# A hybrid block on one core: the gating branch ahead of the attention, its two projections as products of 2x2 blocks

## The chip, the core and the metric

One core of a Trainium2 chip runs the whole kernel. The time is device microseconds of one execution; the number for a kernel is the median of its runs. The engines are TensorE (PE, with its weight loads PEld), VectorE (DVE), ScalarE (ACT), GpSimd (POOL) and SyncE (SP), whose queue issues all the DMAs of this kernel.

## The reference

One layer over 512 positions of 1024 channels, all in float32. The parts that matter here:

```python
h = rmsnorm(x, norm_mix_g)
z = einsum('bsd,dc->bsc', h, w_in)              # 1024 -> 7184 columns
uv = gelu(z[..., :2048]); z_u, z_v = uv[..., :1024], uv[..., 1024:]
q, k, v, f_logit = ...                          # 3 x 1024 columns, 16 columns
gate_a, gate_b = split(sigmoid(z[..., 5136:]))  # 2 x 1024 columns
a = z_u * (mask(w_s) @ layernorm(z_v) + b_s)    # blocks of 128 positions, 8 groups
b = forgetting_attention(q, k, v, f_logit, b_f) # 16 heads, causal, cumsum of log sigmoid
x = x + (gate_a * (a @ w_a) + gate_b * (b @ w_b)) @ w_out
```

A gated MLP with a causal convolution, an embedding add and a last norm follow; the change doesn't touch them.

## The kernel before

Every product of the projections keeps float32 accuracy by a split. An operand is cast to the PE's float32r format (`hi`, on ACT) and the rest is subtracted (`lo`, on DVE or POOL); three matmuls (hi·lo, lo·hi, hi·hi) stand for one. `load_w` does it for a weight tile of 512 KB: a DMA into a `raw` buffer, the cast (L127), the subtraction (L128). `hT` holds the normed input, transposed and split, in two slots. A projection of 512 columns is four row blocks by 8 contraction tiles by 3 = 96 matmuls of 128x512.

PE's order is the program's (written out by hand in blocks, or by the order of the code). The other engines' order is set by a scheduler from the same code, and each engine then executes its queue strictly in order. A ring gives the weight buffers: 5 pairs of `whi`/`wlo` and 3 of `raw`. A load is issued on SP when its raw buffer is free. PSUM has 8 banks, in tags that rotate; a matmul that starts a bank waits until its last content has been read.

The stages: (1) x is normed in four blocks (`rms_x`, with `gmix`, the norm's weights copied to all partitions by POOL, L336) and transposed into hT, while PE does the embedding's product (`pp`) and the first half of V (`pv`). (2) The forget gate's 16 matmuls (L410) and its cumsum, a scan of nine steps on DVE (L424, L425). (3) The second half of V (`proj_N`, 96 matmuls). (4) Attention by 8 pairs of heads, with the projections of q and k and 13 of the 16 gate tiles woven in; the gates go to DRAM (`gate_d`). (5) The zv projection (192 matmuls), layernorm of zv on DVE and POOL (L693 to L696), the zu projection (192). (6) The w_b phase, with the remaining gates and the mix of group g (`mix`: 3 matmuls with w_s, 4 transposes, into `aT`) between its tiles; then w_a, w_out and the rest.

Of the kernel before, what the change touches and what calls it, by code (L numbers as in the profile page):

```python
# [9 lines left out]
F32 = mybir.dt.float32  # L10
F32R = mybir.dt.float32r
# [4 lines left out]
P = 128  # L16
# [22 lines left out]
def hybrid_block(  # L39
# [27 lines left out]
    def uid(s):  # L67
        state["n"] += 1
        return f"{s}_{state['n']}"
# [26 lines left out]
    LATE = ("qy", "qt", "qh", "st", "mv", "va", "s0", "s1", "s2", "s3")  # L96
# [126 lines left out]

    ident = consts.tile([P, P], F32, tag="ident", name="ident")
# [89 lines left out]
    ring = open_ring("ring", 5)  # L314
# [10 lines left out]
    with tc.manual_schedule(engines={ET.PE, ET.Activation, ET.DVE, ET.SP}):  # L325
# [10 lines left out]
        G.partition_broadcast(gmix, grow)  # L336
# [60 lines left out]


    bft = consts.tile([P, 1], F32, tag="bft", name="bft")
    nc.sync.dma_start(bft[0:16, :], b_f.rearrange("o h -> h o"))  # L400

    wf_raw = scr.tile([P, 8, 64], F32, tag="wfr", name="wf_raw")
    wf2 = scr.tile([P, 8, 64], F32R, tag="wf2", name="wf2")
    nc.sync.dma_start(wf_raw, w_in_v[:, :, 5120:5184])
    V.tensor_copy(wf2, wf_raw)
    V.tensor_tensor(wf2[:, :, 32:48], wf_raw[:, :, 0:16], wf2[:, :, 0:16].bitcast(F32), ALU.subtract)
    bk = bank()
    for k in range(8):
        for t in (1, 0):
            T.matmul(bk[0:64, :], wf2[:, k, :], hT[t][:, k, :],  # L410
                     start=(k == 0 and t == 1), stop=(k == 7 and t == 0))
    fz = scr.tile([16, S], F32, tag="fz", name="fz")
    fa = scr.tile([16, S], F32, tag="fa", name="fa")
    fb = scr.tile([16, S], F32, tag="fb", name="fb")
# [16 lines left out]
    state["bank"] = 0  # L431
    proj_N(w_in_v[:, :, 4096:5120], 0, NK, hT, 1, evac_v, rb_outer=False)

# [5 lines left out]
    scr_es.close()  # L439
    psum.close()  # L440


    psum = open_psum("psumB", ATT_BANKS)
# [108 lines left out]


    gate_d = tc.dram_tile([N_EARLY * P, S], F32, name="gate_d")

    def gate_col(n):
        return (6160 if n < NK else 5136) + P * (n % NK)

    def gate_early(n):
        w = load_w(w_in_v[:, :, gate_col(n):gate_col(n) + P], 8, P, sub=None)  # L560
        bk = bank("mm")
        yield from proj_T_steps([(*w, 0, 8, 0)], hT, bk)
        t = att.tile([P, S], F32, tag="ot", name=uid("gt"), bufs=1)
        A.copy(t, bk)
        nc.sync.dma_start(gate_d[n * P:n * P + P, :], t)
# [6 lines left out]
    def run(g):  # L572
        for _ in g:
            pass

    def weave(items, fill, n):

        steps = len(items)
        done = 0
        for m, g in enumerate(items):  # L580
            next(g, None)
            while done < (m + 1) * n // steps:
                next(fill, None)
                done += 1

    def chain(*gs):
        for g in gs:
            yield from g

    with tc.manual_schedule(engines={mybir.EngineType.PE}):  # L590
# [3 lines left out]
        fill = chain(qk_pair(1, qk_weights(1), qk[1]), gate_early(0))  # L594
# [32 lines left out]
    state["pool"][5] = state["pool"][6] = state["pool"][7] = state["late"] = late  # L627
    scr_es, scr = open_pool("scrC", "right")

    zv = slot(5, F32).rearrange("p (b c) -> p b c", b=NB)  # L630

    def evac_zv(bk, rb, ch):
        state["zv"] = A.activation(zv[:, rb, 512 * ch:512 * ch + 512], bk, AF.Gelu_apprx_tanh)

    state["bank"] = 1
# [3 lines left out]
    prep = slot(7, F32)  # L639
    gb = prep[:, 1024:3072].rearrange("p (a c) -> p a c", a=2)  # L640
    nc.sync.dma_start(gb[:, 0, :], rows_bc(ln_g[0], D))
    nc.sync.dma_start(gb[:, 1, :], rows_bc(ln_b[0], D))


    wst = prep[:, 0:1024].rearrange("p (g s) -> p g s", g=8)
    nc.sync.dma_start(wst, w_s[0].rearrange("g t s -> t g s"))
    G.memset(wst[0:64, :, 64:128], 0.0)
    wsT = tuple(scr.tile([P, 8, P], F32R, tag=f"wsT{i}", name=f"wsT{i}") for i in range(2))
    for g0 in (0, 4):
        bk = bank()  # L650
        for g in range(4):
            T.transpose(bk[:, g * P:(g + 1) * P], wst[:, g0 + g, :], ident)
        split_out(wsT, bk.rearrange("p (g t) -> p g t", g=4),
                  (slice(None), slice(g0, g0 + 4), slice(None)))


    cvr = [prep[:, 3072 + P * i:3072 + P * i + P] for i in range(2)]
# [7 lines left out]
    nc.sync.dma_start(cvr[1][88:96, :], b_s[0])  # L665
    cvT = late.tile([P, 2 * P], F32, tag="cvT", name="cvT")
    late.tile([P, 32], F32, tag="gap", name="gap_late")
    bk = bank()
    for i in range(2):
        T.transpose(bk[:, i * P:(i + 1) * P], cvr[i], ident)  # L670
    V.tensor_copy(cvT, bk[:, :2 * P])
# [8 lines left out]
    def bs(g):  # L680
        return cvT[:, P + 88 + g:P + 89 + g]

    mv = tiny("mv", 2 * NB)
    va = tiny("va", NB)
    for rb in range(NB):
        st = tiny("st", 12)
        for h in range(2):
            V.bn_stats(st[:, 6 * h:6 * h + 6], zv[:, rb, 512 * h:512 * h + 512])
        V.bn_aggr(mv[:, 2 * rb:2 * rb + 2], st)
        V.tensor_scalar(va[:, rb:rb + 1], mv[:, 2 * rb + 1:2 * rb + 2], EPS, None, ALU.add)  # L690
    y = rsqrt_of(va, NB)
    for rb in range(NB):
        V.tensor_scalar(zv[:, rb, :], zv[:, rb, :], mv[:, 2 * rb:2 * rb + 1], y[:, rb:rb + 1],  # L693
                        ALU.subtract, ALU.mult)
        G.tensor_tensor(zv[:, rb, :], zv[:, rb, :], gb[:, 0, :], ALU.mult)
        G.tensor_tensor(zv[:, rb, :], zv[:, rb, :], gb[:, 1, :], ALU.add)  # L696

    zu = slot(6, F32).rearrange("p (b c) -> p b c", b=NB)

    def evac_zu(bk, rb, ch):  # L700
        A.activation(zu[:, rb, 512 * ch:512 * ch + 512], bk, AF.Gelu_apprx_tanh)

    oT = tuple(k_view(slot(i)) for i in (2, 3))
    with tc.issue_after(state["zv"].ins):
        for c in range(NK):
            split_out(oT, o32[:, c, :], (slice(None), c, slice(None)))
    aT = tuple(k_view(slot(i)) for i in (7, 4))

    def mix(g):
        c = slice(g * P, g * P + P)  # L710
        vh = scr.tile([P, NB, P], F32R, tag="vh", name=uid("vh"), bufs=1)
        vl = scr.tile([P, NB, P], F32R, tag="vl", name=uid("vl"), bufs=1)
        split_out((vh, vl), zv[:, :, c], (slice(None),) * 3)
        bk = bank()
        mm3(bk, wsT[0][:, g, :], wsT[1][:, g, :], vh, vl, True, True)
        an = scr.tile([P, NB, P], F32, tag="an", name=uid("an"), bufs=1)
        V.scalar_tensor_tensor(an, bk.rearrange("p (b c) -> p b c", b=NB), bs(g),
                               zu[:, :, c], ALU.add, ALU.mult)
        bk = bank()
        for n in range(NB):  # L720
            T.transpose(bk[:, n * P:(n + 1) * P], an[:, n, :], ident)
        split_out(aT, bk, (slice(None), g, slice(None)))

    for ch in range(2):
        proj_N(w_in_v[:, :, 0:1024], 0, NK, hT, ch, evac_zu, rb_outer=False)


    def gated(wv, act, n0):

        c0 = P * (n0 % NK)  # L730
        sgs = []
        for i in range(2):
            sg = scr.tile([P, S], F32, tag="sg", name=uid("sg"), bufs=2)
            if n0 + i < N_EARLY:
                nc.sync.dma_start(sg, gate_d[(n0 + i) * P:(n0 + i + 1) * P, :])
                src = sg
            else:
                src = bank()
                w = load_w(w_in_v[:, :, gate_col(n0 + i):gate_col(n0 + i) + P], 8, P)
                proj_T([(*w, 0, 8, 0)], hT, src)  # L740
            A.activation(sg, src, AF.Sigmoid)
# [263 lines left out]
```

## Time and profile before

| | before |
|---|---|
| median of 3 runs | 971.17 us (970.8 to 971.34) |
| profiled execution | 971.98 us, span 970.2 us |
| mean granted PE clock | 0.994 |
| PE busy | 946.9 us of the span |
| DVE, ACT, POOL busy | 559.6, 433.5, 139.3 us |
| moved by DMA | 110.72 MB, 114 GB/s |

The median is what counts as the time. The span runs from the first to the last instruction of the profiled execution. Busy time adds up the instructions' own durations, with what overlaps on an engine counted once.

### The profile page before, as it was taken

How to read it: one execution, taken by the hardware profiler on the slowest of the kernel's cores; microseconds unless marked ns; L12 is line 12 of the kernel's file. 1: busy time of each engine (PE TensorE's matmuls, PEld its weight loads, DVE VectorE, ACT ScalarE, POOL GpSimd, SP SyncE). 2: the span in 40 equal slices, each digit the busy share in tenths (PEclk: the TensorE clock that was granted, in tenths of full speed). 3: DMA queues.
4: the chain of work that ended last, by engine and by line, in shares of the span. 5: the costliest groups of instructions: out<-in, count | busy, mean ns of one | idle time of the engine just before them, and what ended most of it. 6: DMA issues, size and time to landing. Idle time of an engine off the chain costs nothing.

```text
span 970.2 us, 11655 instructions
## 1 busy us (share of the span) xinstructions
PE 946.9 (98%) x4422; PEld 785.1 (81%) x4422; DVE 559.6 (58%) x982; ACT 433.5 (45%) x721; POOL 139.3 (14%) x99
## 2 busy tenths in 40 slices
PE   6999999999999999999999999999999999999996
PEld 4778888878888888888888888888888888888885
DVE  4464877788852495454634756565356653365664
ACT  5355666666643353333423544343234341244443
POOL 1203222230000036000310400000000000000225
PEclk8999999999999999999999999999999999999998
DMA  5544433333236324556552333224223333223202
GB/s 184 174 118 145 114 102 99 98 94 101 90 98 178 109 65 130 161 165 212 184 200 66 112 119 95 87 87 130 88 66 111 106 109 89 85 87 124 72 22 87
DMA packets 96725, 110.72 MB, mean 114 GB/s; under 512 B 4821, under 2 KB 70541, under 8 KB 96670
## 3 DMA queue, kind: packets, MB, share of 16 engines
q1 hardware_dynamic: 96526, 109.72, 36.5%
q8 instruction: 35, 0.57, 0.3%
q10 hardware_dynamic: 144, 0.26, 0.1%
q14 instruction: 20, 0.16, 0.1%
HBM read 101.29 MB, written 8.68 MB: 113 GB/s over the span
## 4 chain that ended last, share of the span: by engine, by line
PE 91%; DVE 3%; POOL 2%; DMA 2%; issue 1%; ACT 1%; SPq 0%; POOLq 0%; DVEq 0%
PE bank L150 17%; PE bank L152 17%; PE bank L154 17%; PE bank L137 8%; PE bank L136 8%; PE bank L138 8%; PE bank L210 3%; PE bank L212 3%; PE bank L214 3%; PE bank L540 2%; PE bank L531 2%; DMA raw<-in_w_in_dram 2%; DVE t L520 1%; PE bank L503 1%; PE bank L269 1%
## 5 line engine op out<-in xcount | busy, mean ns | idle before, releaser
L150 PE MATMUL bank<-slot,wlo 128*128 128x512 f32 (+1 forms) x744 | 294.3, 397 | 0.0
L152 PE MATMUL bank<-slot,whi 128*128 128x512 f32 (+1 forms) x744 | 289.0, 389 | 0.0
L154 PE MATMUL bank<-slot,whi 128*128 128x512 f32 (+1 forms) x744 | 288.6, 388 | 0.0
L128 DVE TENSOR_TENSOR wlo<-raw,whi 128x1024 fp32r<-128x1024 f32 x132 | 173.7, 1318 | 139.8 <-ACT whi L127 139.3
L127 ACT CAST whi<-raw 128x1024 fp32r<-128x1024 f32 x156 | 163.2, 1047 | 175.8 <-PE bank L138 115.5
L154 PEld LDWEIGHTS bank<-slot,whi 128*128 128x128 f32 x744 | 139.6, 188 | 28.8
L150 PEld LDWEIGHTS bank<-slot,wlo 128*128 128x128 f32 x744 | 140.0, 188 | 23.7
L152 PEld LDWEIGHTS bank<-slot,whi 128*128 128x128 f32 x744 | 140.1, 188 | 22.3
L136 PE MATMUL bank<-whi,slot 128*128 128x512 f32 (+1 forms) x360 | 138.4, 385 | 0.0
L138 PE MATMUL bank<-whi,slot 128*128 128x512 f32 (+1 forms) x360 | 138.4, 384 | 0.0
L137 PE MATMUL bank<-wlo,slot 128*128 128x512 f32 (+1 forms) x360 | 138.4, 384 | 0.0
L128 POOL TENSOR_TENSOR wlo<-raw,whi 128x1024 fp32r<-128x1024 f32 x24 | 58.6, 2446 | 482.8 <-ACT whi L127 465.2
L136 PEld LDWEIGHTS bank<-whi,slot 128*128 128x128 f32 x360 | 67.6, 188 | 13.5
L138 PEld LDWEIGHTS bank<-whi,slot 128*128 128x128 f32 x360 | 67.6, 188 | 13.5
L137 PEld LDWEIGHTS bank<-wlo,slot 128*128 128x128 f32 x360 | 67.6, 188 | 13.3
L210 PE MATMUL bank<-whi,slot 128*128 128x512 f32 x152 | 60.3, 397 | 2.8 <-DVE slot L234 2.1
L212 PE MATMUL bank<-wlo,slot 128*128 128x512 f32 x152 | 59.3, 391 | 2.9 <-POOL wlo L128 2.9
L214 PE MATMUL bank<-whi,slot 128*128 128x512 f32 x152 | 59.7, 392 | 0.0
L845 DVE SCALAR_TENSOR_TENSOR ul<-bank,cvT,ul 128x511 f32<-128x511 f32 x22 | 16.5, 750 | 51.7 <-ACT ul L844 51.7
L234 DVE TENSOR_TENSOR slot<-bank,slot 128x512 fp32r<-128x512 f32 x42 | 27.9, 685 | 28.4 <-ACT slot L233 28.2
L513 ACT ACTIVATE t<-t,mn 128x512 f32<-128x512 f32 (+1 forms) x64 | 35.9, 562 | 11.7 <-DVE mn L510 7.9
L210 PEld LDWEIGHTS bank<-whi,slot 128*128 128x128 f32 x152 | 28.6, 188 | 9.9 <-DVE slot L234 3.3
(175 smaller groups left out, 1032.7 us busy)
## 6 DMA issues: line engine op xcount, KB each, us to landing
raw<-in_w_in_dram SPq DMA_DIRECT2D x56, 512.0 KB, 4.0
raw<-in_w_up_dram SPq DMA_DIRECT2D x44, 512.0 KB, 3.6
raw<-in_w_down_dram SPq DMA_DIRECT2D x22, 512.0 KB, 3.4
cum<-cum_d SPq DMA_DIRECT2D x8, 512.0 KB, 4.0
raw<-in_w_branch_b_dram SPq DMA_DIRECT2D x8, 512.0 KB, 4.6
raw<-in_w_branch_a_dram SPq DMA_DIRECT2D x8, 512.0 KB, 6.7
raw<-in_w_out_dram SPq DMA_DIRECT2D x8, 512.0 KB, 5.6
raw<-in_w_ple_gate_dram SPq DMA_DIRECT2D x8, 512.0 KB, 3.3
```

What stands on the lines that cost most here:

```text
L127: A.copy(hi, raw)
L128: (sub or V).tensor_tensor(lo, raw, hi.bitcast(F32), ALU.subtract)
L136: T.matmul(out_ap, alo, bhi, start=start, stop=False)
L137: T.matmul(out_ap, ahi, blo, start=False, stop=False)
L138: T.matmul(out_ap, ahi, bhi, start=False, stop=stop)
L150: T.matmul(out_ap, wl, ah, start=(n == 0 and k == 0), stop=False)
L152: T.matmul(out_ap, wh, al, start=False, stop=False)
L154: T.matmul(out_ap, wh, ah, start=False, stop=end)
L210: T.matmul(bk, alo[:, k, r], wh, start=(k == 0), stop=False)
L212: T.matmul(bk, ahi[:, k, r], wl, start=False, stop=False)
L214: T.matmul(bk, ahi[:, k, r], wh, start=False, stop=(k == nk - 1))
L513: A.activation(t, t, AF.Exp, scale=-1.0, bias=m, accum_out=rs[:, i:i + 1])
```

## The change

The gating branch moves ahead of the attention. Its two projections, zv and zu, 512x1024 by 1024x1024 each, are computed as 2x2 blocks by seven block products (Strassen's scheme in Winograd's form). The sums S1 to S4 of quarters of hT are made once, on POOL and DVE, and split. The sums of the weights' quarters are made on POOL in the raw buffers (`combine`, two operations 128x1024 for each of four sums and each projection); each product then has two weight tiles to cast (ACT) and subtract (DVE, `split_w`), and 24 matmuls into two banks (two row blocks, 4 contraction tiles, 3). Additions from PSUM on DVE put the products together.

The rest of the change follows from it. gmix comes by a DMA that repeats the row on all partitions, and POOL no longer does it. The first ring has 4 pairs and 8 raw buffers. The scan and the sums stand in the code ahead of V's second half. The layernorm's statistics are sums on ACT, its multiplication one DVE operation (L677) and its addition one POOL operation for each row block. The mix follows zu and is woven with three gate tiles; its `aT` goes to DRAM (`aT_d`) and is read back, 4 MB, behind the attention. The attention opens a new ring and new PSUM banks and weaves 12 gate tiles in; one more gate tile and the splits of the attention's output stand between it and the w_b phase, which reads all 16 gates from DRAM.

```diff
-GATES = [1, 2, 3, 4, 5, 6, 7, 10, 13]
-N_EARLY = GATES[-1]
+GATES = [4, 5, 6, 7, 8, 9, 10, 12, 15]
+N_MIX = GATES[0] - 1
+N_GATES = 2 * NK
+WINO_BANKS = {"c": 6, "f": 2}
...
+        t3 = lambda: combine((0, 1), (1, 1), (0, 1), ALU.subtract)
+        t2 = lambda: combine((0, 0), (0, 1), (0, 0), ALU.add)
+        t1 = lambda: combine((0, 1), (1, 1), (0, 0), ALU.subtract)
+        t4 = lambda: combine((1, 0), (1, 0), (0, 0), ALU.subtract)
...
+            (ready((0, 0), load), product("P1", act, 0, 0, "x", True)),
+            (ready((0, 1), t3), product("P7", sums[2], 0, 0, "z", True)),
+            (ready((0, 0), t2), product("P6", sums[1], 0, 0, "y", True)),
+            (ready((1, 0), t1), product("P2", act, 4, 0, "x", False)),
+            (ready((0, 1), t4), product("P5", sums[0], 0, 0, "y", False)),
+            (ready((1, 0)), product("P4", act, 4, 256, "z", False)),
+            (ready((1, 1)), product("P3", sums[3], 0, 0, "y", False)),
...
+            if name == "P1":
+                A.copy(c12, bk)
+            elif name == "P7":
+                V.tensor_tensor(c22, bk, c12, ALU.add)
...
-    ring = open_ring("ring", 5)
+    ring = open_ring("ring0", 4, 8)
...
-        grow = scr.tile([1, D], F32, tag="grow", name="grow")
-        nc.sync.dma_start(grow, norm_mix_g)
-        G.partition_broadcast(gmix, grow)
+        nc.sync.dma_start(gmix, rows_bc(norm_mix_g[0], D))
...
+    add_quarter(s1, a21, 1, 1, ALU.add)
+    split_out(sums[0], s1, full)
+    G.tensor_tensor(a21, a11, a21, ALU.subtract)
+    split_out(sums[2], a21, full)
...
+            V.scalar_tensor_tensor(zv[:, rb, :], zv[:, rb, :], y[:, rb:rb + 1], gb[0],
+                                   ALU.mult, ALU.mult)
+            G.tensor_tensor(zv[:, rb, :], zv[:, rb, :], gb[1], ALU.add)
+        steps(units, 120)
+        wsT = [quarter(f"S1{t}").rearrange("p (g t) -> p g t", g=8) for t in "hl"]
...
+        bk = bank("f")
+        T.transpose(bk[:, 0:P], bsr, ident)
+        V.tensor_copy(bsT, bk[:, 0:NK])
+        steps(units, 24)
...
+            for t in range(2):
+                nc.sync.dma_start(aT_d[t][g * P:g * P + P, :], ap[:, t].bitcast(F32))
...
+    ring = open_ring("ring", 5)
     psum = open_psum("psumB", ATT_BANKS)
...
-    proj_N(w_in_v[:, :, 1024:2048], 0, NK, hT, 0, evac_zv, rb_outer=False)
-    proj_N(w_in_v[:, :, 1024:2048], 0, NK, hT, 1, evac_zv, rb_outer=False)
...
-    for ch in range(2):
-        proj_N(w_in_v[:, :, 0:1024], 0, NK, hT, ch, evac_zu, rb_outer=False)
...
-        for g in range(c0 // P, c0 // P + 2):
-            mix(g)
```

The first place is DVE around V's second half. `slot_30` and `slot_31` hold V, and the four rows that write them from a bank are the evacuations of its row blocks; `fa` and `fb` before, and `mid_449` and `mid_450` now, are the scan's two tiles. Before:

```order
L128 TENSOR_TENSOR wlo_734<-raw_732,whi_733 128x1024 [waits DMAHW0_49,Activation_49]
L424 COPY fb<-fa 16x64 [waits DVE_49]
L425 TENSOR_TENSOR fb<-fa 16x448
L424 COPY fa<-fb 16x128 [waits DVE_49]
L425 TENSOR_TENSOR fa<-fb 16x384
L424 COPY fb<-fa 16x256 [waits DVE_49]
L425 TENSOR_TENSOR fb<-fa 16x256
L128 TENSOR_TENSOR wlo_740<-raw_738,whi_739 128x1024 [waits DMAHW1_49,Activation_49]
L234 TENSOR_TENSOR slot_30_135<-bank_515,slot_30_135 128x8x64 [waits Activation_49]
L234 TENSOR_TENSOR slot_30_135<-bank_516,slot_30_135 128x8x64 [waits Activation_49]
L234 TENSOR_TENSOR slot_31_136<-bank_517,slot_31_136 128x8x64 [waits Activation_49]
L234 TENSOR_TENSOR slot_31_136<-bank_518,slot_31_136 128x8x64 [waits Activation_49]
```

Now, with `zv_448` the scratch of the sums, `S4l` the low part of the sum S4, and `wlo_707` the low part of the second product's weights:

```order
L560 COPY mid_449<-mid_450 16x8 [waits DVE_49]
L561 TENSOR_TENSOR mid_449<-mid_450 16x504
L560 COPY mid_450<-mid_449 16x16 [waits DVE_49]
L561 TENSOR_TENSOR mid_450<-mid_449 16x496
L236 TENSOR_TENSOR wlo_707<-raw_688,whi_706 128x1024 [waits Activation_49]
L560 COPY mid_449<-mid_450 16x32 [waits DVE_49]
L561 TENSOR_TENSOR mid_449<-mid_450 16x480
L351 TENSOR_TENSOR slot_30_133<-bank_550,slot_30_133 128x8x64 [waits Activation_49]
L351 TENSOR_TENSOR slot_30_133<-bank_551,slot_30_133 128x8x64 [waits Activation_49]
L560 COPY mid_450<-mid_449 16x64 [waits DVE_49]
L561 TENSOR_TENSOR mid_450<-mid_449 16x448
L351 TENSOR_TENSOR slot_31_134<-bank_552,slot_31_134 128x8x64 [waits Activation_49]
```

The evacuations stood behind the scan and between weight splits; now the first two stand behind the sums and most of the scan, and the third, of `bank_552`, one scan step further on. The first product's second bank, `bank_715`, takes the place of `bank_552`.

The second place is DVE right behind the last step of the layernorm's inverse root (`qy`). Before, in the zu projection (`vl` is the first mix's):

```order
L693 TENSOR_SCALAR slot_626_2924<-slot_626_2924,mv_3215,qy_3237 128x1024 [waits DVE_49]
L693 TENSOR_SCALAR slot_626_2924<-slot_626_2924,mv_3215,qy_3237 128x1024 x3
L128 TENSOR_TENSOR wlo_3427<-raw_3425,whi_3426 128x1024 [waits DMAHW1_49,Activation_49]
L128 TENSOR_TENSOR wlo_3433<-raw_3431,whi_3432 128x1024 [waits DMAHW2_49,Activation_49]
L128 TENSOR_TENSOR wlo_3550<-raw_3548,whi_3549 128x1024 [waits DMAHW3_49,PE_49,Activation_49]
L128 TENSOR_TENSOR wlo_3556<-raw_3554,whi_3555 128x1024 [waits DMAHW4_49,Activation_49]
L234 TENSOR_TENSOR vl_3615<-slot_626_2924,vh_3614 128x512 [waits Activation_49]
```

Now, in zu's last two products; `wlo_1225` and `wlo_1229` are the weights of the last product, P3, `wlo_1318` and `wlo_1399` those of gates, and `S1l_1261` the low part of the transposed w_s:

```order
L677 SCALAR_TENSOR_TENSOR zv_671<-zv_671,qy_1053,mid_978 128x1024 [waits DMAHW6_49,DVE_49]
L677 SCALAR_TENSOR_TENSOR zv_671<-zv_671,qy_1053,mid_978 128x1024 x3
L236 TENSOR_TENSOR wlo_1225<-raw_930,whi_1224 128x1024 [waits DMAHW5_49,Activation_49]
L330 TENSOR_TENSOR slot_117_672<-bank_1124,slot_117_672 128x512 [waits PE_49]
L330 TENSOR_TENSOR slot_117_672<-bank_1125,slot_117_672 128x512 [waits PE_49]
L236 TENSOR_TENSOR wlo_1229<-raw_932,whi_1228 128x1024 [waits DMAHW6_49,Activation_49]
L130 TENSOR_TENSOR wlo_1318<-raw_1316,whi_1317 128x1024 [waits DMAHW3_49,Activation_49]
L333 TENSOR_TENSOR slot_117_672<-bank_1086,slot_117_672 128x512 [waits PE_49]
L333 TENSOR_TENSOR slot_117_672<-bank_1087,slot_117_672 128x512 [waits PE_49]
L130 TENSOR_TENSOR wlo_1399<-raw_1397,whi_1398 128x1024 [waits DMAHW4_49,Activation_49]
L351 TENSOR_TENSOR S1l_1261<-bank_1262,S1h_1260 128x512 [waits Activation_49]
```

PE's transpose of `bsr` writes the bank that `bank_1262` had, and stands in PE's order ahead of P3; so P3 stands behind the last of these rows. Before, no matmul of zu needed a bank whose reading stood behind the layernorm's rows.

The third place is SP at the start of the attention's loads. Before, the first weights of q and k are `raw_654` and `raw_660`, in V's second half:

```order
L124 DMA raw_503<-in_w_in_dram 128x2x512 [waits DMAHW4_49,Pool_49]
L124 DMA raw_509<-in_w_in_dram 128x2x512 [waits DMAHW5_49,DMAHW0_49,DVE_49]
L124 DMA raw_654<-in_w_in_dram 128x8x128 [waits DMAHW6_49,DMAHW3_49,DVE_49]
L124 DMA raw_660<-in_w_in_dram 128x8x128 [waits DMAHW7_49,DMAHW4_49,DVE_49]
L124 DMA raw_732<-in_w_in_dram 128x8x128 [waits DMAHW5_49,DVE_49]
L124 DMA raw_738<-in_w_in_dram 128x8x128 [waits DMAHW6_49,DMAHW1_49,DVE_49]
L124 DMA raw_853<-in_w_in_dram 128x8x128 [waits DMAHW7_49,DMAHW2_49,DVE_49]
```

Now they are `raw_1592` and `raw_1598`, behind the stores of the mix (`S4h`, `S4l` are reused for its result):

```order
L711 DMA aT_d_676<-S4h_1534 128x512 [waits DMAHW4_49,Activation_49]
L711 DMA aT_d_677<-S4h_1534 128x512 [waits DMAHW5_49,DVE_49]
L711 DMA aT_d_676<-S4l_1548 128x512 [waits DMAHW6_49,Activation_49]
L126 DMA raw_1592<-in_w_in_dram 128x8x128 [waits DMAHW7_49]
L711 DMA aT_d_677<-S4l_1548 128x512 [waits DMAHW0_49,DVE_49]
L626 DMA gate_d<-mid_1558 128x512 [waits DMAHW1_49,Activation_49]
L126 DMA raw_1598<-in_w_in_dram 128x8x128 [waits DMAHW2_49]
L126 DMA raw_1670<-in_w_in_dram 128x8x128 [waits DMAHW3_49]
L773 DMA cum_1666<-cum_d 128x1024 [waits DMAHW4_49,PE_49]
```

The loads of the first pair moved from V's second half to the end of the mix, between the stores of its last group.

More of the change, by code (lines that the diff above doesn't have):

```diff
@@ L406, in hybrid_block @@
     V.tensor_tensor(wf2[:, :, 32:48], wf_raw[:, :, 0:16], wf2[:, :, 0:16].bitcast(F32), ALU.subtract)
+    state["bank"] = 3
     bk = bank()
[L408 to L414, printed above, removed]
+    with tc.manual_schedule(engines={ET.PE}):
+        for k in range(8):
+            for t in (1, 0):
+                T.matmul(bk[0:64, :], wf2[:, k, :], hT[t][:, k, :],
+                         start=(k == 0 and t == 1), stop=(k == 7 and t == 0))
+    fz, fa, fb = fm[0][0:16, 0:512], fm[0][0:16, 512:], fm[1][0:16, 0:512]
     A.copy(fa, bk[32:48, :])
@@ new lines, in gelu_zu, with gate_col, gate_steps @@
+    def gelu_zu(src, rb, h):
+        A.activation(zu[:, rb, 512 * h:512 * h + 512], src, AF.Gelu_apprx_tanh)
+    gate_d = tc.dram_tile([N_GATES * P, S], F32, name="gate_d")
+    def gate_col(n):
+        return (6160 if n < NK else 5136) + P * (n % NK)
+    def gate_steps(n, tag, place):
+        w = load_w(w_in_v[:, :, gate_col(n):gate_col(n) + P], 8, P, sub=None)
+        bk = bank(tag)
+        yield from proj_T_steps([(*w, 0, 8, 0)], hT, bk)
+        t = place()
+        A.copy(t, bk)
+        nc.sync.dma_start(gate_d[n * P:n * P + P, :], t)
@@ new lines, in run, with weave, chain @@
+    def run(g):
+        for _ in g:
+            pass
+    def weave(items, fill, n):
+        steps = len(items)
+        done = 0
+        for m, g in enumerate(items):
+            next(g, None)
+            while done < (m + 1) * n // steps:
+                next(fill, None)
+                done += 1
+    def chain(*gs):
+        for g in gs:
+            yield from g
+    bsT = ph.tile([P, NK], F32, tag="bsT", name="bsT")
+    aT_d = [tc.dram_tile([D, S], F32, name=f"aT_d{t}") for t in range(2)]
@@ L550, in av_head @@
         yield
-    gate_d = tc.dram_tile([N_EARLY * P, S], F32, name="gate_d")
-    def gate_col(n):
-        return (6160 if n < NK else 5136) + P * (n % NK)
     def gate_early(n):
[L560 to L565, printed above, removed]
+        return gate_steps(n, "mm", lambda: att.tile([P, S], F32, tag="ot", name=uid("gt"), bufs=1))
     qk = [[] for _ in range(NPAIR)]
@@ L754, in hybrid_block @@
             nc.sync.dma_start(gyb_d[c * P:c * P + P, :], sg)
-        for g in range(c0 // P, c0 // P + 2):
-            mix(g)
+    bk = bank()
+    for i in range(2):
+        T.transpose(bk[:, i * P:(i + 1) * P], cvr[i], ident)
+    V.tensor_copy(cvT, bk[:, :2 * P])
     mT = tuple(k_view(slot(i)) for i in (5, 2))
```

290 lines of the change are left out of this document (198 added, 92 removed).

## The prediction, made before the changed kernel was run

> **What bounds the kernel now.** I read the head of the page and the granted clock first, then the engines by stretches, then the timeline wherever TensorE (PE) stands still.
>
> ```profile
> span 970.2 us, 11655 instructions
> PE 946.9 (98%) x4422; PEld 785.1 (81%) x4422; DVE 559.6 (58%) x982; ACT 433.5 (45%) x721; POOL 139.3 (14%) x99
> ```
>
> The first row is the page's span, the second the busy time of each engine. PE is the bound, 98% of the span. The table by stretches says the same of every stage (columns: stretch, its length, busy time and instructions of PE, weight loads, DVE, ACT, POOL, the granted PE clock, DMA share, GB/s):
>
> ```profile
> 12.00:14.00 2.00, 0.00 (x0) 0.00 (x0) 0.00 (x0) 0.72 (x2) 0.76 (x1) 0.64 1.08 353
> 16.00:18.00 2.00, 2.00 (x9) 1.88 (x8) 1.82 (x2) 1.13 (x3) 0.00 (x0) 0.50 0.00 0
> 18.00:20.00 2.00, 2.00 (x7) 1.54 (x6) 1.72 (x6) 1.97 (x5) 0.00 (x0) 0.65 0.00 0
> 298.00:341.00 43.00, 43.00 (x191) 35.59 (x190) 14.63 (x20) 16.49 (x20) 0.88 (x3) 1.00 0.52 151
> 343.00:386.00 43.00, 43.00 (x192) 35.55 (x191) 33.59 (x38) 17.09 (x25) 24.06 (x8) 1.00 0.31 94
> 386.00:455.00 69.00, 69.00 (x321) 57.12 (x320) 32.31 (x41) 24.70 (x35) 0.00 (x0) 1.00 0.59 186
> ```
>
> The zv projection (298 to 341), the zu projection (343 to 386) and the w_b phase behind them have no idle PE. So a matmul removed there is worth its pitch, as long as nothing new makes PE wait. The same rows say what has room: DVE is busy 15 of 43 us in zv and 34 of 43 in zu, POOL 1 and 24. The pitch comes from the first and the last of zv's 192 matmuls; the durations in such rows overlap, so 0.39 isn't the price of one:
>
> ```profile
> 297.81 0.39 PE L136 MATMUL bank<-whi,slot 128*128 128x512 f32 x1
> ...
> 341.10 0.39 PE L138 MATMUL bank<-whi,slot 128*128 128x512 f32 x1
> 341.33 1.03 PE L652 MATMUL bank<-ident,slot 128*128 128x128 f32 x8
> 342.20 0.38 PE L670 MATMUL bank<-ident,slot 128*128 128x128 f32 x2
> ```
>
> (341.10 − 297.81) / 191 = 0.2266 us. Eight transposes take 342.20 − 341.33 = 0.87 us.
>
> PE does wait in the first 50 us:
>
> ```profile
> 7.50 0.50 PE L210 MATMUL bank<-whi,pT 128*128 128x512 f32 x1 [0.20 <-DVE pT L234]
> 13.24 1.30 POOL L336 PARTITION_BROADCAST gmix<-grow  x1 [11.30 <-issue]
> 14.58 1.41 DVE L280 SCALAR_TENSOR_TENSOR hn<-xs,ry,gmix 128x512 f32<-128x512 f32 x2 [4.68 <-POOL gmix L336]
> 15.48 1.94 PE L269 MATMUL bank<-ident,hn 128*128 128x128 f32 x8 [4.92 <-DVE hn L280]
> 24.26 0.50 PE L212 MATMUL bank<-wlo,slot 128*128 128x512 f32 x1 [2.87 <-POOL wlo L128]
> 28.89 1.04 ACT L127 CAST whi<-raw 128x1024 fp32r<-128x1024 f32 x1 [6.06 <-DMA raw<-in_w_in_dram]
> 29.04 0.48 SPq L124 DMA_DIRECT2D raw<-in_w_in_dram  x1
> 52.95 3.84 PE L410 MATMUL bank<-slot,wf 128*64 128x512 f32 x16
> ```
>
> PE waits 4.92 us for the broadcast of gmix, then runs at clock 0.50 until about 19.4, then waits 2.87 us for a POOL split. ACT waits 6.06 us for a raw weight, because three raw buffers hold the queue back.
>
> **The change, part by part.**
>
> *Matmuls.* Each projection has 7 products of 24 matmuls in place of 192 matmuls: 336 against 384, or 48 × 0.2266 = −10.9 us. The mix, the gates, the attention's matmuls and the two transposes of cvr are moved, not saved; one transpose (bsr) is new, 0.1 us, taken as nothing.
>
> *Start-up.* gmix comes by DMA, and eight raw buffers let the weights through without waiting for splits. In the rows above the waits of the two causes are 4.92 and some 2 us for the slow clock behind it, 2.87, and what follows ACT's 6.06. Up to 52.95, from 7.50 on, PE has 128 matmuls (29.0 us) and 32 transposes (3.2 us), so it loses 45.4 − 32.2 = 13.2 us. One POOL split (2.4 us) and one chain of statistics (some 1.5 us) stay in the way: I take −9, with the ends −5 (only gmix's wait goes) and −13 (everything goes).
>
> *The first product.* PE's first product of zv uses two banks. Its second one reuses the bank of V half 1's third row block, and that block's evacuation stands on DVE behind the sums S1 to S4 and the scan (order of DVE, above in the section on the change). The prices:
>
> ```profile
> L128 DVE TENSOR_TENSOR wlo<-raw,whi x132: 1204/1225/3425, 5.5 to 939.1; 128x1024 fp32r<-128x1024 f32 x132
> L128 POOL TENSOR_TENSOR wlo<-raw,whi x24: 2332/2404/2854, 21.9 to 916.4; 128x1024 fp32r<-128x1024 f32 x24
> L128 DVE TENSOR_TENSOR wlo<-raw,whi x4: 3051/3408/3425, 360.6 to 371.0; 128x1024 fp32r<-128x1024 f32 x4
> 354.55 11.71 POOL L695 TENSOR_TENSOR slot<-slot,slot 128x1024 f32<-128x1024 f32 x4 [42.26 <-DVE slot L693]
> 366.23 12.38 POOL L696 TENSOR_TENSOR slot<-slot,slot 128x1024 f32<-128x1024 f32 x4
> 353.50 7.16 DVE L693 TENSOR_SCALAR slot<-slot,mv,qy 128x1024 f32<-128x1024 f32 x4
> L693 DVE TENSOR_SCALAR slot<-slot,mv,qy x4: 806/1852/2893, 353.5 to 357.8; 128x1024 f32<-128x1024 f32 x4
> L425 DVE TENSOR_TENSOR fb<-fa 16x511 f32<-16x511 f32 (+4 forms) x5 | 3.0, 602 | 0.0
> L424 DVE COPY fb<-fa 16x1 f32<-16x1 f32 (+4 forms) x5 | 0.9, 184 | 0.1
> L234 DVE TENSOR_TENSOR slot<-bank,slot 128x512 fp32r<-128x512 f32 x42 | 27.9, 685 | 28.4 <-ACT slot L233 28.2
> 57.71 0.73 DVE L416 SCALAR_TENSOR_TENSOR fz<-bank,bft,fa 16x512 f32<-16x512 f32 x1
> ```
>
> The first three rows give min/median/max in ns. The third is the same DVE split between 360 and 375 us, beside the POOL rows below it: 3.41 us in place of 1.22. POOL's 2.40 us and DVE's 1.22 add up to 3.62, so the two nearly exclude each other. It costs the kernel before nothing, since PE has prepared work there. The Trainium skill states this as a rule ("SBUF — State Buffer", section "Who interferes with whom"): a DVE instruction with two SBUF inputs and a GpSimd instruction that reads SBUF lock each other out for a whole instruction. The trace agrees, by 3.41 against 1.22 us, and the rule speaks against this change, which puts 23 reading POOL operations beside such DVE work (3 for the sums, 16 combines, 4 in the LN), where 8 stood before (L695, L696).
>
> From the last matmul of V half 0 to that evacuation DVE has twelve operations 128x1024 with two SBUF inputs (12 × 1.22 = 14.6), seven scan steps (7 × 0.79 = 5.5), two small ones (1.5) and four evacuations (2.8); POOL has five (5 × 2.40 = 12.0) that exclude the twelve. Together 36.4 us. PE's cover is 16 + 96 + 6 matmuls: 118 × 0.2266 = 26.7 us. A stall of +10; without exclusion DVE needs 24.4 and it is 0; with a sixth POOL operation before it, 12. The third product's second half may wait too; by DVE's rows +1 (0 to 2).
>
> *zu's last product (P3).* The LN runs while PE does zu's products. Behind the inverse root DVE has four 128x1024 multiplications that alternate with POOL's four additions, four weight splits, four additions from PSUM, and then S1l, whose bank the transpose of bsr takes, and PE executes P3 only behind that. The nearest row is L693, 7.16 us for four beside POOL's L695; the new form has two SBUF inputs, 1.41 us for 1024 columns (two of L280) against 0.81 for L693's fastest, so 7.16 + 4 × 0.60 = 9.6. One split beside POOL 3.4, one half beside it 2.1, two free 2.4, four PSUM additions 2.8, S1l 0.7: 21.0 us. PE's cover is P4 (24 × 0.2266 = 5.4) and eight transposes (0.9), 6.3, if the root ends as P4 starts: 14.7. It stands right behind the split of P4's second weights and may end a little sooner: I take +13. Without exclusion 4 × 1.41 + 4 × 1.22 + 2.8 + 0.7 = 14.0, less 6.3 and less what the root gains, 4 to 8; if the root ends later, 17.
>
> *The way into the attention.* Before, its first weights are loaded and split during V half 1. Now the first load stands on SP behind a store of the last mix, and the last step of the mix has only gates to cover it (5 matmuls, 1.1 us, are left). The chain: copy of the last block 0.58, issue 0.5, landing 4.0, cast 1.05, split 1.22, less 1.1 = 6.3. The rows for the copy and for the landing (the issue is in the start-up's rows):
>
> ```profile
> L564 ACT COPY gt<-bank 128x512 f32<-128x512 f32 x13 | 7.6, 587 | 12.3 <-PE bank L154 5.7 <-DVE slot L549 5.6 <-ACT t L513 1.0
> raw<-in_w_in_dram SPq DMA_DIRECT2D x56, 512.0 KB, 4.0
> ```
>
> The softmax of the first pair is then uncovered for some 1.2 us more: +8 (6 to 10).
>
> *Clock.* Behind the 4.92 us wait above the clock fell to 0.50 and stayed there until about 19.4, some 3.9 us, of which half is lost. Three stalls of 8 to 13 us: up to 3 × 2 = 6; I take +5 (0 to 8). The Trainium skill ("TensorE: Matmul & The Clock Gate", Part 1) puts the drop at one idle window of about 3.4 us and the return at one busy window of about 3.4 us; the rows 12 to 20 agree with it, and by it the estimate for three stalls would be 3 × 1.7 = 5.1.
>
> *After the attention.* oT's splits now have one gate (24 matmuls, 5.4 us) for cover, but most pairs are done earlier, and w_b begins with the first four; the 4 MB of aT and 4 MB of gates come by DMA in phases whose share was 0.59 of the DMA engines at 186 GB/s. I cost it at nothing; the cover is PE's 24 matmuls for each tile of w_b. The POOL combines of the other products and the 28 splits go beside PE: seven products of 5.44 us give 38.1, DVE's 14 × 1.22 + 10 × 0.69 = 24.0 and POOL's 8 × 2.40 = 19.2 together 43: nearly full, and a stall of 5 over a projection isn't excluded (in the range).
>
> *Sum.* −10.9 − 9 + 10 + 1 + 13 + 8 + 5 = +17.1. The profiled execution took 971.98 us (970.2 of span), 0.8 over the median 971.17. 971.98 + 17.1 = 989.1, or 988 for the median.
>
> **Rivals.**
>
> *No collision: faster.* If DVE and POOL pass one another, the first product's wait is 0, P3's 5, and one or two stalls stay: −10.9 − 9 + 0 + 0 + 5 + 8 + 2 = −4.9, 966. Against it is 3.41 beside 1.22. It decides from the point at which the exclusion costs less than 1.2 us of the 2.4 for each of the POOL operations; for it speaks that POOL's L696 took 3.1 apiece, not 3.6, so that some of the time does overlap.
>
> *DMA after the attention.* 4 MB of aT, 2 MB of gates and 4 MB of weights in w_b's 192 matmuls (43.5 us) is 230 GB/s through one queue; the rows above show 353 at the start, but landings of 6.7 us where w_a's weights came with others. If eight loads come 1.5 us late each: +12, 1000. Against: the loads have three buffers of lead.
>
> ```profile
> raw<-in_w_branch_a_dram SPq DMA_DIRECT2D x8, 512.0 KB, 6.7
> ```
>
> *The start-up gains little.* The 512 KB of gmix share the queue with x and the weights at 353 GB/s, 1.5 us; if it lands late and the POOL split stays in the way, the gain is −3: 994.
>
> **How the numbers follow.** The forecast with its neighbours 0.55, the DMA rival 0.12, the small start-up gain 0.10, no collision 0.18, all else near zero 0.05. The likeliest is 988, its own range 978 to 998. The 8-in-10 range takes in no collision's upper part and the DMA rival: 966 to 1003. A measurement of this kernel can't tell under 0.2% (2 us) from no change: slower 0.77, same 0.05, faster 0.18.
>
> **What would show it.** The matmuls of the two projections: 336 at 0.227 pitch. First transposes of hn before 13 us, and the forget gate's matmuls at about 44 rather than 52.95. One PE idle time of 7 to 12 us in front of the first product's second bank, put down to DVE; one of 9 to 15 us in front of bsr's transpose or P3; one of 6 to 10 us at the first attention matmul, put down to a weight's cast or split; splits of 2.5 to 3.5 us on DVE wherever POOL combines. The prediction is wrong if these splits stay at 1.2 us, if the evacuations come before the sums, or if idle PE appears in the w_b and w_a phases.

## The result, and the profile after

The changed kernel takes 998.13 us (median of 4 runs, 997.01 to 1000.25) against 970.98 (970.71 to 971.34): a ratio of 1.028, with the 95% interval 1.026 to 1.030. It is slower by 27 us. One execution of `before_start`, further down, ran at a mean clock of 0.654 and took 1355.58 us; it is left out of that kernel's numbers. The page's head and the granted clock of the profiled execution:

```profile
span 995.5 us, 11761 instructions
PE 945.6 (95%) x4375; PEld 780.7 (78%) x4375; DVE 608.8 (61%) x1012; ACT 461.6 (46%) x771; POOL 183.4 (18%) x114
core 0: 995.5 us, clock 0.978
```

PE has 47 instructions fewer (48 matmuls less, one transpose more) and yet nearly the same busy time, 945.6 us against 946.9, since more of it ran at the slow clock; and its share fell from 98% to 95% of a longer span. DVE is busy for 49 us more, POOL for 44, with the time in which they hold each other up. PE's timeline shows the start and then four places at which it waits (the last bracket is the idle time before the instruction and what ended it):

```profile
10.85 1.23 PE L386 MATMUL bank<-ident,hn 128*128 128x128 f32 x8 [0.18 <-DVE hn L397]
42.34 3.84 PE L548 MATMUL bank<-slot,mid 128*64 128x512 f32 x16
67.58 0.39 PE L283 MATMUL bank<-whi,slot 128*128 128x512 f32 x1
...
80.42 0.79 PE L283 MATMUL bank<-whi,slot 128*128 128x512 f32 x1 [11.32 <-DVE slot L351]
135.61 0.51 PE L283 MATMUL bank<-whi,S2l 128*128 128x512 f32 x1 [2.23 <-ACT whi L235]
136.87 0.79 PE L287 MATMUL bank<-wlo,S2h 128*128 128x512 f32 x1 [0.75 <-DVE wlo L236]
170.55 0.48 PE L690 MATMUL bank<-ident,bsr 128*128 128x128 f32 x1 [12.23 <-DVE S1l L351]
210.62 0.77 PE L152 MATMUL bank<-slot,wlo 128*128 128x512 f32 x1 [7.04 <-DVE wlo L130]
```

The first transposes of hn no longer wait for gmix, and V's second half ends at 67.58 where it ended at 76.60: 9.0 us gained. Then come 11.32 us ahead of the first product's second bank, 3.0 us in zu's third product (its weights' cast and split), 12.23 us ahead of bsr's transpose, and 7.04 us ahead of the first attention matmul. Behind each the clock is at half for a while (columns as in the table by stretches of before):

```profile
70.00:80.00 10.00, 0.00 (x0) 0.00 (x0) 9.97 (x12) 1.00 (x2) 7.30 (x3) 0.59 0.00 0
80.00:90.00 10.00, 9.58 (x32) 7.68 (x33) 6.78 (x9) 3.26 (x5) 2.89 (x2) 0.73 0.42 110
420.00:520.00 100.00, 100.00 (x447) 82.75 (x446) 36.49 (x45) 34.46 (x50) 7.30 (x5) 1.00 0.73 240
```

PE stands still from 70 to 80 while DVE is busy without a break. From 80.4 on eleven matmuls came at a pitch of 0.43 us in place of 0.227, 2.4 us; with the same count behind the other three waits (1.4, 1.7 and 2.1) it is 7.6 us. Behind the attention, in w_b and w_a, PE has no idle time although 240 GB/s are moved.

Why DVE is late shows in its own timeline and POOL's, here from the sums (48 to 55 us) and the scan (69 to 75):

```profile
48.28 3.41 DVE L351 TENSOR_TENSOR S3l<-zv,S3h 128x1024 fp32r<-128x1024 f32 x1
51.62 3.41 DVE L351 TENSOR_TENSOR S1l<-zv,S1h 128x1024 fp32r<-128x1024 f32 x1
...
69.49 2.30 DVE L560 COPY mid<-mid 16x8 f32<-16x8 f32 x1
72.42 2.19 DVE L560 COPY mid<-mid 16x16 f32<-16x16 f32 x1
47.29 6.65 POOL L256 TENSOR_TENSOR raw<-raw,raw 128x1024 f32<-128x1024 f32 x2 [5.15 <-DVE slot L351]
64.30 10.28 POOL L256 TENSOR_TENSOR raw<-raw,raw 128x1024 f32<-128x1024 f32 x2 [10.36 <-DVE wlo L236]
```

While POOL adds quarters of weights (L256), splits of 1.22 us take 3.41, and a copy of 16 by 8 numbers takes 2.30 us in place of 0.15. POOL suffers too: two of its additions take 10.28 us in place of 4.8. In zu the same, with the layernorm (min/median/max in ns where a row counts several; the ACT row is from its timeline):

```profile
L665 DVE TENSOR_TENSOR nm<-zs x1: 2351/2351/2351, 123.4 to 123.4; 128x4 f32<-128x4 f32 x1
L666 DVE TENSOR_SCALAR nm<-nm x1: 2314/2314/2314, 125.8 to 125.8; 128x4 f32<-128x4 f32 x1
128.17 4.27 ACT L669 ACTIVATE zv<-zv,nm 128x1024 f32<-128x1024 f32 x4 [4.52 <-DVE nm L666]
L677 DVE SCALAR_TENSOR_TENSOR zv<-zv,qy,mid x4: 1280/2336/3422, 150.7 to 156.5; 128x1024 f32<-128x1024 f32 x4
L679 POOL TENSOR_TENSOR zv<-zv,mid x4: 3314/3336/3374, 152.1 to 162.0; 128x1024 f32<-128x1024 f32 x4
```

### The profile page after: what moved, and what is told of

The parts are those of the page before. It is cut to its first block, busy times and chain, and to the rows that moved or that the text cites. A ratio compares the mean times of both kernels' runs of the same rounds, so it can differ in the third digit from the quotient of the medians.

```text
span 995.5 us, 11761 instructions
## 1 busy us (share of the span) xinstructions
PE 945.6 (95%) x4375; PEld 780.7 (78%) x4375; DVE 608.8 (61%) x1012; ACT 461.6 (46%) x771; POOL 183.4 (18%) x114
## 5 line engine op out<-in xcount | busy, mean ns | idle before, releaser
L130 DVE TENSOR_TENSOR wlo<-raw,whi 128x1024 fp32r<-128x1024 f32 x116 | 145.2, 1255 | 115.0 <-ACT whi L129 114.6
L129 ACT CAST whi<-raw 128x1024 fp32r<-128x1024 f32 x140 | 145.9, 1046 | 130.4 <-PE bank L140 69.2
L138 PE MATMUL bank<-whi,slot 128*128 128x512 f32 (+1 forms) x232 | 89.4, 386 | 0.1
L140 PE MATMUL bank<-whi,slot 128*128 128x512 f32 (+1 forms) x232 | 89.1, 384 | 0.0
L139 PE MATMUL bank<-wlo,slot 128*128 128x512 f32 (+1 forms) x232 | 89.0, 383 | 0.0
L256 POOL TENSOR_TENSOR raw<-raw,raw 128x1024 f32<-128x1024 f32 x16 | 48.3, 3029 | 49.6 <-DVE wlo L236 32.6
L236 DVE TENSOR_TENSOR wlo<-raw,whi 128x1024 fp32r<-128x1024 f32 x28 | 47.7, 1713 | 10.5 <-ACT whi L235 10.5
L138 PEld LDWEIGHTS bank<-whi,slot 128*128 128x128 f32 x232 | 43.6, 188 | 9.4 <-DVE slot L351 0.5
L140 PEld LDWEIGHTS bank<-whi,slot 128*128 128x128 f32 x232 | 43.6, 188 | 9.2
L139 PEld LDWEIGHTS bank<-wlo,slot 128*128 128x128 f32 x232 | 43.6, 188 | 9.1
L235 ACT CAST whi<-raw 128x1024 fp32r<-128x1024 f32 x28 | 29.2, 1050 | 30.8 <-PE bank L290 28.6
```

The lines of the kernel that those rows point to most:

```text
L129: A.copy(hi, raw)
L130: (sub or V).tensor_tensor(lo, raw, hi.bitcast(F32), ALU.subtract)
L138: T.matmul(out_ap, alo, bhi, start=start, stop=False)
L139: T.matmul(out_ap, ahi, blo, start=False, stop=False)
L140: T.matmul(out_ap, ahi, bhi, start=False, stop=stop)
L256: G.tensor_tensor(d, u, v, op)
```

## The experiments

All are set against the kernel before, run beside each of them (970.8 to 971.2 us); "the wait" is PE's idle time as in the timeline above. The theory is that POOL's reading operations and DVE's work exclude each other, and that PE stands behind DVE's queue; its rivals are that only the order of DVE's queue counts, or only the amount of DVE's work, or that moving the branch ahead is what costs.

**Without the additions on POOL.**

```diff
-            for d, u, v in zip(B[dst], B[a], B[b]):
-                G.tensor_tensor(d, u, v, op)
+            return
```

> The changed kernel (998.1) without the 16 POOL additions that combine the weights' quarters; the products read the quarters as loaded, all else is issued as before, DVE in the same order. Theory (POOL and two-input DVE work exclude each other): the wait before the first product's second bank falls from 11.3 to about 2 us, the wait in zu's third product from 3 us (with slow clock 5) to 1 to 3, the one before bsr's transpose stays near 11 because the layernorm's POOL additions stay; with the slow clock that goes with them 984 to 987. Rival (only the place in DVE's queue and the amount of DVE work count): all waits stay, 996 to 999.

Measured: 981.98 us (979.67 to 982.44), ratio 1.0117 [1.010, 1.013]: 16 us less, more than expected. DVE's order was the same. Its timeline of PE, and the scan's copies:

```profile
71.25 0.50 PE L282 MATMUL bank<-whi,slot 128*128 128x512 f32 x1 [1.78 <-DVE slot L350]
153.25 0.48 PE L689 MATMUL bank<-ident,bsr 128*128 128x128 f32 x1 [11.43 <-DVE S1l L350]
L559 DVE COPY mid<-mid x9: 134/161/272, 60.1 to 72.3; 16x1 f32<-16x1 f32 x1, 16x2 f32<-16x2 f32 x1, 16x4 f32<-16x4 f32 x1, 16x8 f32<-16x8 f32 x1
```

The first wait fell from 11.32 to 1.78, the one in zu's third product is gone, and no copy takes over 0.27 us. The wait for bsr stayed, as it should. The order of DVE's queue alone can't be the cause of the first two. Leaving the additions out also drops the step in which a cast waits for an addition; but that can't have delayed the evacuation, since in the changed kernel DVE worked without a pause from 61.2 us until the evacuation was done, and its two waits just before (2.45 and 0.72 us, for ACT) are as long here.

**Nothing on POOL beside zu.** The layernorm's POOL additions are left out as well (`G.tensor_tensor(zv[:, rb, :], ..., gb[1], ALU.add)`).

> As nocombine (982.0), and the layernorm's four POOL additions of its bias left out too, so that POOL reads nothing beside zu. Theory (exclusion): DVE's four multiplications take 5.6 us in place of 9.1, the two splits behind them 2.4 in place of 5.5, and the wait before bsr's transpose falls from 11.4 to 4 to 6 us: 974 to 977. Rival (the chain's own length): 980 to 982.

Measured: 975.05 us (974.63 to 976.32), ratio 1.0043 [1.003, 1.006], as the theory had it.

```profile
147.18 0.48 PE L688 MATMUL bank<-ident,bsr 128*128 128x128 f32 x1 [5.23 <-DVE S1l L350]
L676 DVE SCALAR_TENSOR_TENSOR zv<-zv,qy,mid x4: 1279/1280/1285, 133.5 to 137.1; 128x1024 f32<-128x1024 f32 x4
```

The wait for bsr is 5.23 in place of 11.43: about 6 of its 12 us are exclusion, the rest the length of DVE's queue. The two runs together put 23 us of the changed kernel's time (998.1 − 975.1) down to POOL's work.

**The additions on DVE.**

```diff
-                G.tensor_tensor(d, u, v, op)
+                V.tensor_tensor(d, u, v, op)
```

> The changed kernel with the 16 additions of weight quarters on DVE instead of POOL. Theory (the shared time of POOL and two-input DVE work bounds zv and zu): an addition takes 1.2 us of it in place of 2.4, 19 us less over both; the waits of 13.9 us in zv and 5.0 in zu fall by half or more: 985 to 991. Rival (DVE's own amount of work bounds): 19.5 us more on DVE, 1003 to 1015.

Measured: 984.45 us (984.13 to 985.33), ratio 1.0136 [1.012, 1.015]: faster by 13.7 us than the changed kernel, and a little better than the theory's range, though DVE has 16 operations more.

```profile
L256 DVE TENSOR_TENSOR raw<-raw,raw x16: 1202/1218/1227, 49.0 to 128.6; 128x1024 f32<-128x1024 f32 x16
72.99 0.50 PE L283 MATMUL bank<-whi,slot 128*128 128x512 f32 x1 [3.12 <-DVE slot L351]
157.39 0.48 PE L690 MATMUL bank<-ident,bsr 128*128 128x128 f32 x1 [12.25 <-DVE S1l L351]
```

An addition that is on the engine which is already late costs less there (1.22 us) than on an idle one that holds it up for 2.4. The rival of DVE's amount of work falls for zv; the wait for bsr is as long as before.

**The scan behind V's evacuations.** The nine steps are queued on DVE behind the last evacuation (`state["so"]` is its instruction).

```diff
+    with tc.issue_after(state["so"].ins):
         while step < S:
             V.tensor_copy(dst[:, 0:step], src[:, 0:step])
```

> The changed kernel with the nine scan steps queued on DVE behind V's evacuations. Theory (the evacuation stands behind the scan, whose steps also wait for POOL): the wait of 11.3 us before the first product's second bank falls to 0 to 3, its slow clock goes, 985 to 989. Rival (DVE as a whole is behind its work): the wait moves to the second or third product, whose weights are split later, and the gain is under 4: 994 to 998.

Measured: 994.12 us (993.75 to 996.8), 4.0 less than the changed kernel: the rival's number.

```profile
66.60 3.37 DVE L351 TENSOR_TENSOR S4l<-zv,S4h 128x1024 fp32r<-128x1024 f32 x1
69.90 3.36 DVE L236 TENSOR_TENSOR wlo<-raw,whi 128x1024 fp32r<-128x1024 f32 x1
75.11 0.80 PE L283 MATMUL bank<-whi,slot 128*128 128x512 f32 x1 [5.70 <-DVE slot L351]
```

The first wait fell only to 5.70, and the one in zu's third product was 3.43 in place of 2.23. What the scan's copies no longer lose to POOL, the two splits that now run in their place lose: 3.37 and 3.36 us, where these two took 1.21 each in the changed kernel.

**The layernorm behind P3's splits, bsr in another bank.** `state["lo"]` is the second split of P3's weights.

```diff
+        with tc.issue_after(state["lo"].ins):
             for rb in range(NB):
                 V.scalar_tensor_tensor(zv[:, rb, :], ...
-        bk = bank("f")
+        bk = bank("c")
         T.transpose(bk[:, 0:P], bsr, ident)
```

> The changed kernel with the layernorm's four multiplications queued on DVE behind the two weight splits of P3, and bsr transposed into another bank. Theory (P3 stands in a queue behind work it doesn't need): the wait of 12.2 us falls to under 1, the mix's first matmul waits 3 to 5 us instead; 988 to 991. Rival (what counts is that the layernorm must end before the mix): the wait only moves behind P3, gain of P3's own 5.4 us at most: 993 to 998.

Measured: 997.32 us (996.16 to 998.02), not to be told from the changed kernel. The wait moved behind P3, to the mix:

```profile
172.17 0.77 PE L138 MATMUL bank<-S2h,S1l 128*128 128x512 f32 x1 [6.84 <-DVE S1l L351]
175.61 0.79 PE L139 MATMUL bank<-S2h,S1h 128*128 128x512 f32 x1 [2.67 <-DVE S2h L351]
```

6.84 and 2.67 in place of 12.23, with a second slow clock between them, and the wait ahead of bsr is gone. The order in the queue set where PE waits; what it waits for is the layernorm's end.

**The last aT stores from ACT's queue.**

```diff
-                nc.sync.dma_start(aT_d[t]...
+                (nc.scalar if g >= 6 else nc.sync).dma_start(aT_d[t]...
```

> The changed kernel with the last two groups' four aT stores issued from ACT's queue, so that the attention's first loads no longer stand behind them on SP. Theory (the loads wait in SP's queue): the wait of 7.0 us before the first attention matmul falls to 0 to 2, its slow clock goes, 989 to 992. Rival (the loads wait for memory that the last gate or mix still holds, or the four stores cost ACT as much): 995 to 998.

Measured: 997.98 us (995.37 to 1000.36). The wait before the attention fell from 7.04 to 3.05, and the time didn't follow. The pair once more:

> The changed kernel once more, for its spread on one chip and beside store_act_again: 997 to 1000, single executions 2 to 3 us apart.

> The same kernel as store_act. If its shorter wait before the attention (3.05 in place of 7.04 us, and half the slow clock) is a gain hidden by the spread, it is 3 to 6 us below after_again; if it is given back elsewhere, within 1.5.

Measured: 997.78 (997.29 to 999.16) and 996.88 (995.24 to 999.19): 0.9 us apart, within their spread. In the profiled execution of `store_act_again`:

```profile
207.70 0.47 PE L152 MATMUL bank<-slot,wlo 128*128 128x512 f32 x1 [3.05 <-DVE wlo L130]
221.59 0.47 PE L152 MATMUL bank<-slot,wlo 128*128 128x512 f32 x1 [2.73 <-DVE st L761]
```

That the loads stood in SP's queue is shown by the shorter wait. It left the clock at full speed, and then a new wait of 2.73 us for the split of the first q (`st`) took about that gain back. The rest was kept in the profiled executions, which are 2.3 and 4.2 us shorter than those of the changed kernel. But the medians are less than 1 apart, and the single executions of `store_act` spread over 5.0 us, those of the changed kernel over 3.2. Why the medians don't show the 4 us stays open.

**The start alone.** The kernel before with gmix by DMA (`before_gmix`), and with three more raw buffers as well (`before_start`):

```diff
-        G.partition_broadcast(gmix, grow)
+        nc.sync.dma_start(gmix, rows_bc(norm_mix_g[0], D))
...
+        if later is not None and len(later) > 1:
+            raw = scr.tile([P, a, b], F32, tag="raw0", name=uid("raw"), bufs=3)
```

> The kernel before (971.0), only with gmix repeated on all partitions by a DMA in place of POOL's broadcast. Theory (the start-up gain of 9.0 us has two parts): the wait of 4.92 us and the slow clock behind it go, the wait for raw weights stays: 963 to 966. Rival (the weights bound the start in any case): 968 to 970.

> The kernel before with the changed kernel's whole start: gmix by DMA, and three more raw buffers for the first five weight tiles. Theory: the second half of V ends 9 us earlier, at 67.6, and nothing is given back later: 961 to 963. Rival (part of the gain is lost where the forget gate or the attention wait for their own loads): 965 to 968.

Measured: 962.51 us (961.81 to 962.73), ratio 0.9910 [0.990, 0.993], and 961.58 us (961.55 to 961.92, three executions), ratio 0.9903 [0.989, 0.992]. gmix alone brings 8.7 us, a little more than expected, and the buffers some 0.9 more. The 6.06 us that ACT waited for a raw weight were for the most part a consequence of the late start: with gmix by DMA alone, its longest such wait is 1.8 us. In `before_gmix`:

```profile
11.28 1.23 PE L269 MATMUL bank<-ident,hn 128*128 128x128 f32 x8 [0.49 <-DVE hn L280]
44.34 3.84 PE L408 MATMUL bank<-slot,wf 128*64 128x512 f32 x16
```

Both beat the kernel before and the changed one.

**The order without the products.** The changed kernel with plain projections in the same place, without the sums and the combines.

```diff
-        units = wino_steps(wino_jobs(w_in_v, 1024, ...) + wino_jobs(w_in_v, 0, ...))
+        units = chain(plain_steps(1024, gelu_zv), plain_steps(0, gelu_zu))
```

> The changed kernel's order (start, gating ahead of the attention, its layernorm and mix) with zv and zu as plain projections of 192 matmuls each, without sums and combines. Theory (the order costs only the wait at the attention's start, 9 us with the slow clock, and pays 9 at the start): 969 to 974, no wait over 2 us in zv and zu; the product scheme itself is then worth +24 to +29. Rival (gating ahead is itself what waits, by its layernorm and mix): 980 or more.

Measured: 981.14 us (980.14 to 981.98), ratio 1.0102 [1.009, 1.012].

```profile
152.64 0.33 PE L682 MATMUL bank<-ident,bsr 128*128 128x128 f32 x1 [2.12 <-DVE S1l L351]
191.15 0.76 PE L152 MATMUL bank<-slot,wlo 128*128 128x512 f32 x1 [6.92 <-DVE wlo L130]
```

My theory put this kernel level with the one before; it is 10 us slower, 19 if the start's gain is counted apart. zv and zu have no wait but the 2.12 us for bsr. The attention's wait with its slow clock (9 us), bsr's, and two of 1.2 and 1.6 us in w_a and w_out make 14 of the 19; about 2 more are matmuls that come a little further apart (next section), and the rest is open. The products themselves cost 998.1 − 981.1 = 17 us, though they have 10.9 us less of matmuls: so waits and slow clock took 28 us.

**Everything at once.** No new lines but those shown above, with the bias additions on DVE and the layernorm's statistics behind the casts of zu's third product.

> The changed kernel with everything at once that took a wait away: the additions of weight quarters and of the layernorm's bias on DVE, the scan behind V's evacuations, P3's splits ahead of the layernorm's multiplications, its statistics behind P6's casts, bsr in another bank, the last aT stores on ACT's queue. Theory (DVE's 47 us of work beside 38 us of matmuls in zu stay over): combine_dve's 984.5 less 4 in zv, less 3 to 6 before the mix, less up to 2 at the attention: 973 to 978, still slower than before. Rival (each wait only moves on): 982 to 986.

Measured: 971.96 us (971.06 to 974.48), ratio 1.0010 [1.000, 1.002]: 26 us less than the changed kernel, a little better than expected, and level with the kernel before, the 9 us of the start included.

```profile
70.20 0.50 PE L283 MATMUL bank<-whi,slot 128*128 128x512 f32 x1 [0.54 <-DVE slot L351]
151.81 0.79 PE L138 MATMUL bank<-S2h,S1l 128*128 128x512 f32 x1 [5.48 <-ACT S2h L350]
185.37 0.47 PE L152 MATMUL bank<-slot,wlo 128*128 128x512 f32 x1 [3.05 <-DVE wlo L130]
199.23 0.47 PE L152 MATMUL bank<-slot,wlo 128*128 128x512 f32 x1 [2.72 <-DVE st L766]
```

The waits in zv are gone, those before the mix and in the attention's beginning are left, one of them (2.72, for the split of q) new against the changed kernel.

## Why the prediction was right, and where its sizes were off

The direction was right, and so were three of the four places at which PE waits; the one in zu's third product was not named. The time lies inside the range of 966 to 1003, 10 us above the likeliest and just at the upper end (998) of the range that the prediction gave its own forecast. Term by term, from the spans (995.5 − 970.2 = +25.3, forecast +17.1):

| term | forecast | measured |
|---|---|---|
| 48 matmuls | −10.9 | −10.9 (PE's count, at the pitch that zv and zu have outside the slow clock) |
| start | −9 | −9.0 (76.60 to 67.58) |
| first product's second bank | +10 | +11.3 |
| zv's third product | +1 | 0 |
| zu's third product | not named | +3.0 |
| bsr and P3 | +13 | +12.2 |
| way into the attention | +8 | +7.0 |
| slow clock | +5 | +7.6 |
| after the attention | 0 | no wait over 1.3 us that wasn't there before |

These add up to +21.2. Of the other 4, some 2.3 are in two stretches, from 520 to 570 (w_a and w_out) and from 818 to 860 (the MLP), in which the matmuls come 0.233 us apart in place of 0.2266, at a granted clock of 1.00: in the 40 us from 818 on PE has 173 matmuls, in the same place before 178. Every kernel here with the gating branch ahead has them, `before_gmix` and `before_start` don't; why is open. The rest are steps that I can't put down to a place.

*Start.* The size was right, the split of it wrong: the prediction named the raw buffers as a second cause, and they are worth 0.9 us of the 9.7 (`before_start` against `before_gmix`). (By its own row of eight, its 32 transposes take 3.5 us, not 3.2; that changes none of its terms.)

*First product.* The mechanism is shown (`nocombine`: 1.78 in place of 11.32). The working was right by its sum rather than in its parts: it priced twelve DVE operations and five of POOL as fully exclusive, and left out that copies of the scan are held up too (2.30 and 2.19 us) and that DVE waited in its order for ACT, which was at the scan's chain (2.45 and 0.72 us). The section "Who interferes with whom" of the Trainium skill's "SBUF — State Buffer" lists copies and `tensor_scalar` among what can lock; the runs here show it for operations of 16 by 8 and 128 by 4 numbers.

*The third products.* The prediction gave +1 to zv's third product, by DVE's rows, and no wait came there. It put nothing on zu's; it only called a stall of 5 us over a projection not excluded, by the sums of DVE's and POOL's work. The wait there was first for ACT. The statistics of zv (a first pass of 4.27 us in one piece, and two of the eight sums of squares) stood ahead of the cast, and had themselves started late, because two operations of 128 by 4 took 2.35 and 2.31 us beside POOL. Without POOL's additions the wait is gone.

*P3.* Size and releaser were right (S1l), the parts too: the four multiplications took 9.13 us where 9.6 were forecast, the split behind them 3.35 where 3.4 were. That bsr's bank was what held P3 up is only half of it: with the bank changed and the splits ahead, nearly the same time was spent behind P3 (`ln_bsr`).

*Slow clock.* Three stalls of up to 2 us each were forecast; four came, and cost 1.4 to 2.4 each. The reading behind the estimate was half right. PE's last matmul ahead of the 4.92 us wait ends at 10.56 in the kernel before, and the clock there (the third number from the end), in a finer table of the same trace, is

```profile
12.00:12.50 0.50, 0.00 (x0) 0.00 (x0) 0.00 (x0) 0.50 (x2) 0.00 (x0) 1.00 1.09 269
12.50:13.00 0.50, 0.00 (x0) 0.00 (x0) 0.00 (x0) 0.22 (x1) 0.00 (x0) 0.56 1.12 365
13.00:13.50 0.50, 0.00 (x0) 0.00 (x0) 0.00 (x0) 0.00 (x0) 0.26 (x1) 0.50 1.06 377
```

So it fell after 2.0 us of standing still, and at the three long waits of the changed kernel after 2.7, 2.2 and 4.7. For the drop these times don't agree with the idle window of about 3.4 us that the prediction cites from the Trainium skill ("TensorE: Matmul & The Clock Gate", Part 1); for the return, 3.9 us after PE starts again, the rows of the prediction come near it. Nor does the length of a wait decide alone: 3.05 us before the attention were followed by the slow clock in `store_act` and not in `store_act_again`.

*The rivals.* "No collision" (966) fell with `nocombine`. DMA after the attention fell with the row 420 to 520: PE 100.00 of 100 us busy at 240 GB/s. The small start-up gain fell with 67.58.

## What to carry to other kernels

Before moving work to an idle engine, ask what it shares with the engine that PE waits for: 16 additions cost 13.7 us less on the busy DVE than on the idle POOL. A saving in matmuls is worth its pitch only if the engines that prepare operands have room in that very stage: zv and zu had 15 and 34 of 43 us on DVE before, and with fewer matmuls and DVE busy for about twice as long (91 us in place of 48 over both, the time in which POOL held it up included) a saving of 10.9 us was paid for with 28 us of waits and slow clock. And change one thing at a time: one DMA in place of a broadcast was worth 8.7 us, nearly the whole gain at the start, and it was hidden inside a change that made the kernel 27 us slower.

## What the hardware showed that I had not expected

A small DVE operation can lose as much beside POOL as a large one: a copy of 16 by 8 took 2.30 us against 0.13 to 0.27 without POOL's work, and a `tensor_scalar` of 128 by 4 took 2.31, while a split of 128 by 1024 took 3.41 in place of 1.22. The two small ones and the split each lost about 2.2 us.
